# One merged matmul for the up projection's two column blocks, fp32 retention values, a residual transposed on VectorE, and tiles on multiples of 512 bytes

## The chip, the cores and the metric

The kernel runs on one core of a Trainium2 chip. The metric is the device time of one execution in microseconds (us); smaller is better. The program is one launch. All inputs lie in HBM as float32, and the output is float32.

## What is computed

One layer of a decoder over 16 learned meta tokens and 256 real tokens (272 in all), model width 2048:

```python
u = rmsnorm(h, attn_norm)
proj = u @ w_in                      # 2048 x 6144: q, k, v of 8 heads; k, q, v, gate of 4 retention heads
ya = rmsnorm(diff_attention(q, k, v), attn_subln) * 0.8
yr = rmsnorm(retention(rq, rk, rv), ret_norm) * silu(rg)
h = h + concat(ya, yr) @ w_out       # 2048 x 2048
u = rmsnorm(h, ffn_norm)
h = h + (silu(causal_conv3(u @ w_gate)) * (u @ w_up)) @ w_down   # 2048 x 5632 twice, 5632 x 2048
return rmsnorm(h, final_norm)[256 real tokens]
```

The weights are read once, 208 blocks of 1 MB in all.

## The kernel before

**Number format.** Every large product is made in three TensorE matmuls of the type fp32r. An operand x is split into a high part (a cast to fp32r) and a low part (x minus the high part, again fp32r), and the product is high·high + high·low + low·high, all added up in PSUM. `prep` (L99 on ScalarE, L100 on VectorE) splits each half block of weights, 128x1024, into `whi` and `wlo`; there are three buffers of each. `load` (L87, on the SP queue) brings a block of 1 MB into one of three `raw` buffers.

**Projections.** `gemm` (L257) makes one block of 128 output features for all tokens: 16 steps k of 128 input features, and in each step three matmuls, L276 `whi`·`hi`, L277 `whi`·`lo`, L278 `wlo`·`hi`. The weights are the stationary operand (128x128, loaded for each matmul), the activations the moving one. Their width is 272 tokens (keys and values), 258 (queries, gates, the output projection, the FFN gate, which needs two tokens more for the convolution) or 256 (the FFN up projection). The activations lie transposed in SBUF, features on partitions: `xhi`, `xlo` for the input projection, `yhi`, `ylo` for the output projection, `ghi`, `glo` for the FFN. `Halves` is a small class that lets one name stand for two tiles of eight steps each. `big`, `wts`, `y`, `att`, `fw` are pools of SBUF; tiles of one tag share a place.

**Order of the work.** Input projection (48 blocks, with the tasks of attention and retention put between matmuls by `pump`), output projection (16 blocks), then for each f of 44 the gate and the up projection, then the down projection. Each engine takes its instructions in order; the framework settles that order when the program is built, from a simulated timeline.

**Retention** (`ret_tasks`). The scores of a head (`rs`, L420, plain fp32) are multiplied by a decay (L422), then split into `sd` (L423) and `sl` (L424); the values are transposed on TensorE and split into `rvh` (L434) and `rvl` (L435); `av` makes three matmuls for each of three key blocks (L448 to L450), twice for each of four heads.

**Output projection** (L551 and on). After each of 16 blocks j, `hT` is the sum of the projection and the residual (L556); its squares, `ghi` (L563) and `glo` (L564) are made from it. A side task transposes two 128x128 pieces of `hT` on TensorE into `ph` (L570), and ScalarE copies them to `htok` (L571), the residual with tokens on partitions, which the down projection needs.

**FFN** (L587 and on). For each f: `g` = gate·`rstd2` (L590), the convolution (L592, L595), `s` = silu (L598), `u` = up·`rstd2` (L601), `u`·`s` (L602), and the split into `fhi` and `flo` (L603, L604). Behind the loop `fn` (the final norm's weights, in the place of `ghi`'s first half) is loaded on the POOL queue (L611) and scaled on VectorE (L616).

**Down projection** (L621 and on). `fhi` or `flo` is the stationary operand, 512 columns of weights the moving one (L629 to L631, PSUM tile `o`). The last six half blocks of the last 512 columns are held back and used in matmuls of 256 columns (`oe`) for the second token block.

**Places in SBUF.** Added up from the tile sizes in the order of allocation, each 128x128 block of `whi` and `wlo` starts 192 bytes past a multiple of 512 bytes (so 64 past a multiple of 128), and each of `fhi` and `flo` on a multiple of 128. A row of `ghi` or `glo` has 258 x 4 = 1032 bytes, so each step k starts 8 bytes further within a line of 128 bytes; a row of `xhi` has 1088 bytes.

Of the kernel before, what the change touches and what calls it, by code (L numbers as in the profile page):

```python
# [10 lines left out]
F32 = mybir.dt.float32  # L11
F32R = mybir.dt.float32r
# [14 lines left out]
NQ = T - Q0  # L27
QT = NQ // 3
KB = [(0, Q0 + QT), (Q0 + QT, Q0 + 2 * QT), (Q0 + 2 * QT, T)]
AH = 8  # L30
# [13 lines left out]
class Halves:  # L44
    def __init__(self, tiles):
        self.tiles = tiles

    def __getitem__(self, ix):
        p, k = ix[0], ix[1]
        return self.tiles[k // HK][(p, k % HK) + tuple(ix[2:])]  # L50


@with_exitstack
def trunk_kernel(ctx, tc, a, out):
# [5 lines left out]
    wp = ctx.enter_context(tc.tile_pool(name="wts", bufs=1))  # L60
    sp = ctx.enter_context(tc.tile_pool(name="small", bufs=2))

    xhi = Halves([big.tile([P, HK, T], F32R, tag=f"acthi{i}", name=f"xhi{i}")
                  for i in range(2)])
    xlo = big.tile([P, KT, T], F32R, tag="actlo", name="xlo")

# [65 lines left out]
    V.memset(ones, 1.0 / D)  # L132
    one = cp.tile([P, P], F32, name="one")
    V.memset(one, 1.0)
    onesr = cp.tile([P, P], F32R, name="onesr")
    V.tensor_copy(out=onesr, in_=one)
    warm = cp.tile([P, 512], BF16, name="warm")
# [118 lines left out]

    def gemm(idx, hi, lo, t0, n, pumps):  # L257
        if idx < 4:
            return first[idx]
        if idx < 6:  # L260
            ps = misc(f"mm{idx}")
        elif idx == 6:
            ps = psx[:, 1]
        else:
            ps = ps1.tile([P, 512], F32, tag="mm", bufs=3, name=f"mm{idx}")
        for half in range(2):
            hf = 2 * idx + half
            ahead(hf)
            whi, wlo = pairs.pop(hf)
            for kk in range(HK):  # L270
                k = half * HK + kk
                wh = whi[:, kk * P:(kk + 1) * P]
                wl = wlo[:, kk * P:(kk + 1) * P]
                xh = hi[:, k, t0:t0 + n]
                xl = lo[:, k, t0:t0 + n]
                PE.matmul(ps[:, :n], wh, xh, start=(k == 0), stop=False)  # L276
                PE.matmul(ps[:, :n], wh, xl, start=False, stop=False)  # L277
                PE.matmul(ps[:, :n], wl, xh, start=False, stop=(k == KT - 1))  # L278
                if kk == HK // 2 - 1 or kk == HK - 1:
                    pump(pumps)  # L280
        return ps

    with ExitStack() as p1:
        yp = p1.enter_context(tc.tile_pool(name="y", bufs=1))
        ap_ = p1.enter_context(tc.tile_pool(name="att", bufs=2))
        yhi = yp.tile([P, KT, NQ], F32R, name="yhi")
        ylo = yp.tile([P, KT, NQ], F32R, name="ylo")

# [113 lines left out]
        def ret_tasks(r, k, q, vs):  # L402
# [3 lines left out]
            dk = [dt_[:KB[0][1], 0], dt_[:QT, 1, :2 * QT], dt_[:QT, 1, 2 * QT:]]  # L406
            sd = [ap_.tile([P, (3 - j) * QT], F32R, tag=f"at{j}", name=f"sd{r}_{j}")
                  for j in range(3)]
            sl = [ap_.tile([P, (3 - j) * QT], F32R, tag=f"sl{j}", name=f"sl{r}_{j}")
                  for j in range(3)]  # L410
            vh = ap_.tile([P, 3, 2 * P], F32R, tag="q2", name=f"rvh{r}")
            vl = ap_.tile([P, 3, 2 * P], F32R, tag="k2", name=f"rvl{r}")
            st = {}

            def scores(j):
                def f():
# [3 lines left out]
                    PE.matmul(ps[:e - b, :n], k[:, b:e], q[:, j * QT:], start=True, stop=True)  # L420
                    t = ap_.tile([P, NQ], F32, tag="kl", name=f"sdf{r}_{j}")
                    V.tensor_tensor(out=t[:e - b, :n], in0=ps[:e - b, :n], in1=dk[j], op=ALU.mult)  # L422
                    S.copy(out=sd[j][:e - b], in_=t[:e - b, :n])  # L423
                    V.tensor_tensor(out=sl[j][:e - b], in0=t[:e - b, :n],  # L424
                                    in1=sd[j][:e - b].bitcast(F32), op=ALU.subtract)
                return f

            def vtr(j):
                def f():
                    b, e = KB[j]  # L430
                    ps = misc(f"rv{r}_{j}")
                    for c in range(2):
                        PE.transpose(ps[:e - b, c * P:(c + 1) * P], vs[c][:, b:e], idt)
                    S.copy(out=vh[:e - b, j], in_=ps[:e - b, :2 * P])  # L434
                    V.tensor_tensor(out=vl[:e - b, j], in0=ps[:e - b, :2 * P],  # L435
                                    in1=vh[:e - b, j].bitcast(F32), op=ALU.subtract)
                return f

            def av(c):
                def f():  # L440
# [4 lines left out]
                    for j, (b, e) in enumerate(KB):  # L445
                        n = e - b
                        o = y[:, c, j * QT:NQ]
                        PE.matmul(o, vh[:n, j, cs], sd[j][:n], start=(j == 0), stop=False)  # L448
                        PE.matmul(o, vh[:n, j, cs], sl[j][:n], start=False, stop=False)
                        PE.matmul(o, vl[:n, j, cs], sd[j][:n], start=False, stop=(j == 2))  # L450
                    q_ = ap_.tile([P, NQ], F32, tag="A", bufs=3, name=f"rsq{r}_{c}")
# [68 lines left out]
        for kind, r in RSEQ:  # L520
# [16 lines left out]
            for c in range(2):  # L537
# [7 lines left out]

        ghi = Halves([big.tile([P, HK, NQ], F32R, tag=f"acthi{i}", name=f"ghi{i}")
                      for i in range(2)])
        glo = big.tile([P, KT, NQ], F32R, tag="actlo", name="glo")
        htok = big.tile([P, 2, D], F32, tag="htok", name="htok")
        acc2 = yp.tile([P, NQ], F32, name="acc2")  # L550
        for j in range(KT):  # L551
# [14 lines left out]

            def htr(j=j, hT=hT):
                ps = misc(f"ph{j}")
                for m in range(2):
                    PE.transpose(ps[:, m * P:(m + 1) * P], hT[:, 2 + m * P:2 + (m + 1) * P], idt)  # L570
                S.copy(out=htok[:, :, j * P:(j + 1) * P],  # L571
                       in_=ps[:, :2 * P].rearrange("p (m c) -> p m c", m=2))
            side.append(htr)
        pump(len(side))
# [7 lines left out]
    with ExitStack() as p2:  # L582
        fp = p2.enter_context(tc.tile_pool(name="ff", bufs=1))
        fw = p2.enter_context(tc.tile_pool(name="fw", bufs=2))
        fhi = fp.tile([P, NF, SEQ], F32R, name="fhi")
        flo = fp.tile([P, NF, SEQ], F32R, name="flo")
        for f in range(NF):  # L587
            ps = gemm(idx, ghi, glo, 0, NQ, 0)
            g = fw.tile([P, NQ], F32, tag="g", name=f"fg{f}")
# [8 lines left out]
            S.activation(out=s, in_=c, func=AF.Silu)  # L598
            ps = gemm(idx + 1, ghi, glo, 2, SEQ, 0)
            u = fw.tile([P, SEQ], F32, tag="u", name=f"fu{f}")  # L600
            V.tensor_tensor(out=u, in0=ps[:, :SEQ], in1=rstd2[:, 2:], op=ALU.mult)  # L601
            V.tensor_tensor(out=u, in0=u, in1=s, op=ALU.mult)  # L602
# [3 lines left out]
            idx += 2  # L606
        fn = big.tile([P, D], F32, tag="acthi0", name="fn")
        endt = big.tile([P, D], F32R, tag="acthi1", name="endt")
        tailt = big.tile([P, 2 * D], F32R, tag="actlo", name="tailt")
        junk = misc("junk")  # L610
# [185 lines left out]
```

## Time and profile before

| | us |
|---|---|
| runs (3) | 1190.66, 1190.8, 1190.87; median 1190.8 |
| the profiled execution | 1190.21 |
| its span, first to last instruction | 1188.4 |

The profiled execution is the one that every row comes from. Its span is 1.8 us shorter than its time. TensorE's matmuls (PE) and its weight loads (PEld) are shown as two engines; DVE is VectorE, ACT ScalarE, SP the engine whose queue issues most DMAs. Matmuls are pipelined and the ends that the trace gives are modelled, so what a matmul costs in a stream is read from the distance between starts and not from its duration.

### The profile page before, as it was taken

How to read it: one execution, taken by the hardware profiler on the slowest of the kernel's cores; microseconds unless marked ns; L12 is line 12 of the kernel's file. 1: busy time of each engine (PE TensorE's matmuls, PEld its weight loads, DVE VectorE, ACT ScalarE, POOL GpSimd, SP SyncE). 2: the span in 40 equal slices, each digit the busy share in tenths (PEclk: the TensorE clock that was granted, in tenths of full speed). 3: DMA queues.
4: the chain of work that ended last, by engine and by line, in shares of the span. 5: the costliest groups of instructions: out<-in, count | busy, mean ns of one | idle time of the engine just before them, and what ended most of it. 6: DMA issues, size and time to landing. Idle time of an engine off the chain costs nothing.

```text
span 1188.4 us, 21369 instructions
## 1 busy us (share of the span) xinstructions
PE 1176.3 (99%) x8847; PEld 1129.8 (95%) x8847; DVE 788.5 (66%) x1413; ACT 559.4 (47%) x871; POOL 2.0 (0%) x7
## 2 busy tenths in 40 slices
PE   9999999999999999999999999999999999999997
PEld 8999999999999999999999999999999988888886
DVE  7888877677776567666666666666666645454544
ACT  7576665544445544444444444444444434343442
POOL 0000000000000000000000000000000000000000
PEclk9999999999999999999999999999999999999998
DMA  8544444444446555555555555455555654555552
GB/s 300 205 156 144 142 145 168 163 156 151 168 150 213 198 187 180 190 192 185 178 180 184 193 190 178 178 184 191 193 179 177 218 207 177 200 189 186 195 188 105
DMA packets 35970, 215.72 MB, mean 182 GB/s; under 512 B 4322, under 2 KB 8650, under 8 KB 11168
## 3 DMA queue, kind: packets, MB, share of 16 engines
q1 hardware_dynamic: 35584, 213.17, 50.8%
q8 instruction: 69, 1.13, 0.4%
q0 software_dynamic: 144, 1.05, 0.3%
q14 instruction: 29, 0.24, 0.1%
q10 hardware_dynamic: 144, 0.14, 0.0%
HBM read 212.24 MB, written 2.10 MB: 180 GB/s over the span
## 4 chain that ended last, share of the span: by engine, by line
PE 95%; DMA 2%; DVE 2%; issue 0%; ACT 0%; SPq 0%; DVEq 0%; ACTq 0%
PE mm L276 24%; PE mm L278 23%; PE mm L277 23%; PE o L631 7%; PE o L629 7%; PE o L630 7%; DMA raw<-in_w_in_dram 2%; PE po L380 1%; DVE wlo L100 1%; DMA raw<-in_w_first_dram 1%; PE sc L330 0%; PE sc L328 0%; DMA xr<-in_x_dram 0%; PE pa L368 0%; PE rs L420 0%
## 5 line engine op out<-in xcount | busy, mean ns | idle before, releaser
L99 ACT CAST whi<-raw 128x1024 fp32r<-128x1024 f32 x381 | 399.7, 1049 | 545.5 <-PE mm L277 300.0
L100 DVE TENSOR_TENSOR wlo<-raw,whi 128x1024 fp32r<-128x1024 f32 x381 | 466.1, 1224 | 267.8 <-ACT whi L99 264.7
L276 PE MATMUL mm<-ghi,whi 128*128 128x258 f32 (+1 forms) x1408 | 396.9, 282 | 0.0
L278 PE MATMUL mm<-ghi,wlo 128*128 128x258 f32 (+1 forms) x1408 | 396.6, 282 | 0.0
L277 PE MATMUL mm<-glo,whi 128*128 128x258 f32 (+1 forms) x1408 | 396.1, 281 | 0.0
L277 PEld LDWEIGHTS mm<-glo,whi 128*128 128x128 f32 x1408 | 266.4, 189 | 0.0
L276 PEld LDWEIGHTS mm<-ghi,whi 128*128 128x128 f32 x1408 | 266.0, 189 | 0.0
L278 PEld LDWEIGHTS mm<-ghi,wlo 128*128 128x128 f32 x1408 | 265.8, 189 | 0.0
L276 PE MATMUL mm<-xhi,whi 128*128 128x272 f32 (+1 forms) x688 | 200.4, 291 | 0.0
L277 PE MATMUL mm<-xlo,whi 128*128 128x272 f32 (+1 forms) x688 | 198.9, 289 | 0.0
L278 PE MATMUL mm<-xhi,wlo 128*128 128x272 f32 (+1 forms) x688 | 197.9, 288 | 0.5 <-DVE wlo L100 0.5
L631 PE MATMUL o<-whi,flo 128*128 128x512 f32 x334 | 131.2, 393 | 0.0
L630 PE MATMUL o<-wlo,fhi 128*128 128x512 f32 x334 | 130.3, 390 | 0.0
L278 PEld LDWEIGHTS mm<-xhi,wlo 128*128 128x128 f32 x688 | 129.5, 188 | 0.8 <-DVE wlo L100 0.7
L276 PEld LDWEIGHTS mm<-xhi,whi 128*128 128x128 f32 x688 | 129.6, 188 | 0.1
L277 PEld LDWEIGHTS mm<-xlo,whi 128*128 128x128 f32 x688 | 129.6, 188 | 0.1
L629 PE MATMUL o<-whi,fhi 128*128 128x512 f32 x334 | 117.8, 391 | 0.0
L630 PEld LDWEIGHTS o<-wlo,fhi 128*128 128x128 f32 x334 | 62.7, 188 | 14.2
L631 PEld LDWEIGHTS o<-whi,flo 128*128 128x128 f32 x334 | 62.7, 188 | 13.5
L629 PEld LDWEIGHTS o<-whi,fhi 128*128 128x128 f32 x334 | 62.7, 188 | 13.1
L276 PE MATMUL mm<-yhi,whi 128*128 128x258 f32 x256 | 73.2, 288 | 0.4 <-ACT whi L99 0.4
L278 PE MATMUL mm<-yhi,wlo 128*128 128x258 f32 x256 | 72.3, 284 | 0.0
(245 smaller groups left out, 1086.5 us busy)
## 6 DMA issues: line engine op xcount, KB each, us to landing
raw<-in_w_in_dram SPq DMA_DIRECT2D x44, 1024.0 KB, 4.9
raw<-in_w_gate_dram SPq DMA_DIRECT2D x44, 1024.0 KB, 4.8
raw<-in_w_up_dram SPq DMA_DIRECT2D x44, 1024.0 KB, 4.8
raw<-in_w_down_dram SPq DMA_DIRECT2D x44, 1024.0 KB, 4.9
raw<-in_w_out_dram SPq DMA_DIRECT2D x16, 1024.0 KB, 4.9
raw<-in_w_first_dram SPq DMA_DIRECT2D x6, 512.0 KB, 8.2
xres<-in_x_dram SPq DMA_DIRECT2D x16, 129.0 KB, 3.9
xr<-in_x_dram SPq DMA_DIRECT2D x6, 273.0 KB, 7.4
```

What stands on the lines that cost most here:

```text
L99: S.copy(out=hi, in_=src)
L100: V.tensor_tensor(out=lo, in0=src, in1=hi.bitcast(F32), op=ALU.subtract)
L276: PE.matmul(ps[:, :n], wh, xh, start=(k == 0), stop=False)
L277: PE.matmul(ps[:, :n], wh, xl, start=False, stop=False)
L278: PE.matmul(ps[:, :n], wl, xh, start=False, stop=(k == KT - 1))
L380: PE.matmul(ps[:QT, i * P:(i + 1) * P], at[j][:n, i - j], vt[:n, j], start=(j == 0), stop=(j == i))
L629: PE.matmul(o, ah, wh, start=start and kk == 0, stop=False)
L630: PE.matmul(o, ah, wl, start=False, stop=False)
L631: PE.matmul(o, al, wh, start=False, stop=stop and kk == 1)
```

## The change

- **Merged up columns.** `ghi` and `glo` of eight steps now lie in one tile `gs[i]`, `[128, 2, 8, 288]`. In the up projection one matmul of 512 columns streams both (two runs of 256 columns) past one load of `whi` and writes 512 PSUM columns; `wlo`·`hi` is added to the first 256. ScalarE copies the second 256 columns to SBUF (`ul`), VectorE adds the first 256 to them. The factor `rstd2` goes to `s`.
- **Plain fp32 retention values.** `sd` and the values (`vt`) stay fp32 and unsplit; one fp32 matmul stands for three fp32r ones.
- **DVE-transposed residual.** VectorE transposes `hT` in blocks of 32x32 into `hb`; four DMAs write it to a scratch tensor `hd` in HBM in token order (runs of 32 floats), and two DMAs in the FFN loop (before f = 8 and f = 16) load it to `htok`.
- **Places.** Pads (`spad`, `cpad`) and the removal of `one` put the weight tiles on multiples of 512 bytes. Activation rows have 288 columns (1152 bytes), the first token that the up projection reads starts on a multiple of 128 bytes (offsets `XO` and `GO`), so that of the 258-column reads 8 bytes ahead of one. `fn` gets a tile of its own in the place of the closed pool `fw`; `endt` and `tailt` take the places of `gs`.

```diff
+TW = 288
+XO = 32 - META
+GO = 30
...
 class Halves:
-    def __init__(self, tiles):
-        self.tiles = tiles
+    def __init__(self, tiles, off, width, lead=()):
+        self.tiles, self.off, self.width, self.lead = tiles, off, width, lead
+        self.per = KT // len(tiles)
...
-        p, k = ix[0], ix[1]
-        return self.tiles[k // HK][(p, k % HK) + tuple(ix[2:])]
+        k = ix[1]
+        c = ix[2] if len(ix) > 2 else slice(0, self.width)
+        return self.tiles[k // self.per][(ix[0],) + self.lead + (
+            k % self.per, slice(c.start + self.off, c.stop + self.off))]
...
+    spad = sp.tile([P, 16], F32, name="spad", bufs=1)
+    dp = ctx.enter_context(tc.tile_pool(name="dram", bufs=1, space=bass.MemoryType.DRAM))
+    xs = [big.tile([P, 2, HK, TW], F32R, tag=f"act{i}", name=f"x{i}") for i in range(2)]
+    xhi, xlo = Halves(xs, XO, T, (0,)), Halves(xs, XO, T, (1,))
...
-    one = cp.tile([P, P], F32, name="one")
+    cpad = cp.tile([P, 80], F32, name="cpad")
...
-    def gemm(idx, hi, lo, t0, n, pumps):
+    def gemm(idx, hi, lo, t0, n, pumps, both=None):
...
-                PE.matmul(ps[:, :n], wh, xh, start=(k == 0), stop=False)
-                PE.matmul(ps[:, :n], wh, xl, start=False, stop=False)
-                PE.matmul(ps[:, :n], wl, xh, start=False, stop=(k == KT - 1))
+                if both is not None:
+                    xb = both[k // HK][:, :, k % HK, GO + t0:GO + t0 + n]
+                    if k == KT - 1:
+                        PE.matmul(ps[:, :n], wl, xh, start=False, stop=False)
+                    PE.matmul(ps[:, :2 * n], wh, xb, start=(k == 0), stop=(k == KT - 1))
+                    if k < KT - 1:
+                        PE.matmul(ps[:, :n], wl, xh, start=False, stop=False)
+                else:
...
-        yhi = yp.tile([P, KT, NQ], F32R, name="yhi")
+        yhi = Halves([yp.tile([P, KT, TW], F32R, name="yhi")], GO, NQ)
...
-                    t = ap_.tile([P, NQ], F32, tag="kl", name=f"sdf{r}_{j}")
-                    V.tensor_tensor(out=t[:e - b, :n], in0=ps[:e - b, :n], in1=dk[j], op=ALU.mult)
-                    S.copy(out=sd[j][:e - b], in_=t[:e - b, :n])
-                    V.tensor_tensor(out=sl[j][:e - b], in0=t[:e - b, :n],
-                                    in1=sd[j][:e - b].bitcast(F32), op=ALU.subtract)
+                    V.tensor_tensor(out=sd[j][:e - b], in0=ps[:e - b, :n], in1=dk[j],
+                                    op=ALU.mult)
...
-                    S.copy(out=vh[:e - b, j], in_=ps[:e - b, :2 * P])
-                    V.tensor_tensor(out=vl[:e - b, j], in0=ps[:e - b, :2 * P],
-                                    in1=vh[:e - b, j].bitcast(F32), op=ALU.subtract)
+                    S.copy(out=vt[:e - b, j], in_=ps[:e - b, :2 * P])
...
-                        PE.matmul(o, vh[:n, j, cs], sd[j][:n], start=(j == 0), stop=False)
-                        PE.matmul(o, vh[:n, j, cs], sl[j][:n], start=False, stop=False)
-                        PE.matmul(o, vl[:n, j, cs], sd[j][:n], start=False, stop=(j == 2))
+                        PE.matmul(o, vt[:n, j, cs], sd[j][:n], start=(j == 0), stop=(j == 2))
...
+        gs = [big.tile([P, 2, HK, TW], F32R, tag=f"act{i}", name=f"g{i}") for i in range(2)]
+        ghi, glo = Halves(gs, GO, NQ, (0,)), Halves(gs, GO, NQ, (1,))
+        hd = dp.tile([SEQ, D], F32, name="hd")
...
-            def htr(j=j, hT=hT):
-                ps = misc(f"ph{j}")
-                for m in range(2):
-                    PE.transpose(ps[:, m * P:(m + 1) * P], hT[:, 2 + m * P:2 + (m + 1) * P], idt)
-                S.copy(out=htok[:, :, j * P:(j + 1) * P],
-                       in_=ps[:, :2 * P].rearrange("p (m c) -> p m c", m=2))
-            side.append(htr)
+            hb = ap_.tile([P, SEQ], F32, tag="t", name=f"hb{j}")
+            V.transpose(out=hb, in_=hT[:, 2:])
+            for i in range(4):
+                c = j * P + i * 32
+                nc.sync.dma_start(
+                    out=hd[:, c:c + 32].rearrange("(b t) f -> t b f", t=32),
+                    in_=hb[i * 32:(i + 1) * 32].rearrange("t (b f) -> t b f", f=32))
...
         for f in range(NF):
+            if f in (8, 16):
+                m = f // 8 - 1
+                nc.sync.dma_start(out=htok[:, m], in_=hd[m * P:(m + 1) * P])
...
-            ps = gemm(idx + 1, ghi, glo, 2, SEQ, 0)
-            u = fw.tile([P, SEQ], F32, tag="u", name=f"fu{f}")
-            V.tensor_tensor(out=u, in0=ps[:, :SEQ], in1=rstd2[:, 2:], op=ALU.mult)
+            V.tensor_tensor(out=s, in0=s, in1=rstd2[:, 2:], op=ALU.mult)
+            ps = gemm(idx + 1, ghi, glo, 2, SEQ, 0, gs)
+            ul = fw.tile([P, SEQ], F32, tag="ul", name=f"ful{f}")
+            S.copy(out=ul, in_=ps[:, SEQ:])
+            u = ul
+            V.tensor_tensor(out=u, in0=ps[:, :SEQ], in1=ul, op=ALU.add)
             V.tensor_tensor(out=u, in0=u, in1=s, op=ALU.mult)
...
-        fn = big.tile([P, D], F32, tag="acthi0", name="fn")
-        endt = big.tile([P, D], F32R, tag="acthi1", name="endt")
-        tailt = big.tile([P, 2 * D], F32R, tag="actlo", name="tailt")
+        p3.close()
+        fnp = p2.enter_context(tc.tile_pool(name="fnp", bufs=1))
+        fn = fnp.tile([P, D], F32, name="fn")
+        endt = big.tile([P, D], F32R, tag="act0", name="endt")
+        tailt = big.tile([P, 2 * D], F32R, tag="act1", name="tailt")
```

## Rows read from the trace of the kernel before

**Rows 1.** The page, part 1: busy us, share of the span and instructions by engine.
```profile
PE 1176.3 (99%) x8847; PEld 1129.8 (95%) x8847; DVE 788.5 (66%) x1413; ACT 559.4 (47%) x871; POOL 2.0 (0%) x7
```

**Rows 2.** Stretches: length, busy us of PE, PEld, DVE, ACT, POOL, clock, DMA share, GB/s.
```profile
352.00:443.00 91.00, 90.56 (x753) 90.29 (x752) 58.06 (x83) 48.06 (x79) 0.00 (x0) 1.00 0.58 205
443.00:941.00 498.00, 498.00 (x4167) 497.45 (x4167) 336.75 (x489) 214.42 (x262) 0.65 (x1) 1.00 0.53 185
941.00:1180.00 239.00, 238.91 (x1080) 197.31 (x1078) 116.87 (x114) 96.90 (x105) 0.00 (x0) 1.00 0.51 180
```

**Rows 3.** Groups by line and form: operands, shapes, count, busy us, mean ns, idle before.
```profile
L276 PE MATMUL mm<-ghi,whi 128*128 128x258 f32 x704 | 199.3, 283 | 0.0
L276 PE MATMUL mm<-ghi,whi 128*128 128x256 f32 x704 | 197.6, 281 | 0.0
L276 PE MATMUL mm<-xhi,whi 128*128 128x272 f32 x416 | 122.0, 293 | 0.0
L276 PE MATMUL mm<-xhi,whi 128*128 128x258 f32 x272 | 78.4, 288 | 0.0
```

**Rows 4.** PE in time order (start, us): first matmul of a gate, an up, a gate.
```profile
663.28 0.28 PE L276 MATMUL mm<-ghi,whi 128*128 128x258 f32 x1
...
669.03 0.28 PE L276 MATMUL mm<-ghi,whi 128*128 128x256 f32 x1
...
674.73 0.28 PE L276 MATMUL mm<-ghi,whi 128*128 128x258 f32 x1
```

**Rows 5.** PE in time order, down projection: two matmuls twelve apart.
```profile
980.13 0.39 PE L629 MATMUL o<-whi,fhi 128*128 128x512 f32 x1
...
982.88 0.39 PE L629 MATMUL o<-whi,fhi 128*128 128x512 f32 x1
```

**Rows 6.** PE in time order, last matmuls: two eight apart, two 44 apart.
```profile
1168.20 0.28 PE L629 MATMUL oe<-whi,fhi 128*128 128x256 f32 x1
...
1169.14 0.28 PE L629 MATMUL oe<-whi,fhi 128*128 128x256 f32 x1
...
1174.53 0.28 PE L630 MATMUL oe<-wlo,fhi 128*128 128x256 f32 x1
...
1179.52 0.28 PE L630 MATMUL oe<-tailt,fhi 128*128 128x256 f32 x1
```

**Rows 7.** PE in time order, input projection: two 272-column matmuls eleven apart.
```profile
299.75 0.29 PE L276 MATMUL mm<-xhi,whi 128*128 128x272 f32 x1
...
301.15 0.29 PE L278 MATMUL mm<-xhi,wlo 128*128 128x272 f32 x1
```

**Rows 8.** PE in time order, output projection: the transposes and what follows them.
```profile
406.56 0.38 PE L570 MATMUL ph<-c_ident,hT 128*128 128x128 f32 x2
406.69 0.37 PE L276 MATMUL mm<-yhi,whi 128*128 128x258 f32 x1
406.90 0.28 PE L277 MATMUL mm<-ylo,whi 128*128 128x258 f32 x1
```

**Rows 9.** PE in time order: retention scores; one half head, first matmul to the next stream.
```profile
253.61 0.89 PE L420 MATMUL rs<-rq,rk 128*100 128x258 f32 x4
...
269.39 0.28 PE L448 MATMUL ro<-sd,rvh 100*128 100x258 f32 x1
...
270.55 0.29 PE L277 MATMUL mm<-xlo,whi 128*128 128x272 f32 x1
```

**Rows 10.** The SP queue in time order, output projection: loads one block apart.
```profile
409.02 0.33 SPq L87 DMA_DIRECT2D raw<-in_w_out_dram  x1
...
415.03 0.33 SPq L87 DMA_DIRECT2D raw<-in_w_gate_dram  x1
```

**Rows 11.** DVE in time order at the end of the FFN loop; in brackets idle, releaser.
```profile
940.35 0.42 DVE L604 TENSOR_TENSOR flo<-fu,fhi 128x256 fp32r<-128x256 f32 x1
942.75 1.23 DVE L616 TENSOR_SCALAR fn<-fn 128x2048 f32<-128x2048 f32 x1 [1.99 <-DMA fn<-in_final_norm_dram]
```

**Rows 12.** The page, part 6: DMA issues, KB each, median us to landing.
```profile
raw<-in_w_out_dram SPq DMA_DIRECT2D x16, 1024.0 KB, 4.9
```

More of the change, by code (lines that the diff above doesn't have):

```diff
@@ L61, in trunk_kernel @@
     sp = ctx.enter_context(tc.tile_pool(name="small", bufs=2))
-    xhi = Halves([big.tile([P, HK, T], F32R, tag=f"acthi{i}", name=f"xhi{i}")
-                  for i in range(2)])
-    xlo = big.tile([P, KT, T], F32R, tag="actlo", name="xlo")
+    spad = sp.tile([P, 16], F32, name="spad", bufs=1)
+    V.memset(spad, 0.0)
+    dp = ctx.enter_context(tc.tile_pool(name="dram", bufs=1, space=bass.MemoryType.DRAM))
+    xs = [big.tile([P, 2, HK, TW], F32R, tag=f"act{i}", name=f"x{i}") for i in range(2)]
+    xhi, xlo = Halves(xs, XO, T, (0,)), Halves(xs, XO, T, (1,))
     chunks = []
@@ L132, in trunk_kernel @@
     V.memset(ones, 1.0 / D)
-    one = cp.tile([P, P], F32, name="one")
-    V.memset(one, 1.0)
+    cpad = cp.tile([P, 80], F32, name="cpad")
+    V.memset(cpad, 0.0)
     onesr = cp.tile([P, P], F32R, name="onesr")
-    V.tensor_copy(out=onesr, in_=one)
+    V.memset(onesr.bitcast(F32), 1.0)
     warm = cp.tile([P, 512], BF16, name="warm")
@@ L275, in gemm @@
                 xl = lo[:, k, t0:t0 + n]
-                PE.matmul(ps[:, :n], wh, xh, start=(k == 0), stop=False)
-                PE.matmul(ps[:, :n], wh, xl, start=False, stop=False)
-                PE.matmul(ps[:, :n], wl, xh, start=False, stop=(k == KT - 1))
+                if both is not None:
[6 more added lines that the diff above has]
+                else:
+                    PE.matmul(ps[:, :n], wh, xh, start=(k == 0), stop=False)
+                    PE.matmul(ps[:, :n], wh, xl, start=False, stop=False)
+                    PE.matmul(ps[:, :n], wl, xh, start=False, stop=(k == KT - 1))
                 if kk == HK // 2 - 1 or kk == HK - 1:
@@ L285, in trunk_kernel @@
         ap_ = p1.enter_context(tc.tile_pool(name="att", bufs=2))
-        yhi = yp.tile([P, KT, NQ], F32R, name="yhi")
-        ylo = yp.tile([P, KT, NQ], F32R, name="ylo")
+        yhi = Halves([yp.tile([P, KT, TW], F32R, name="yhi")], GO, NQ)
+        ylo = Halves([yp.tile([P, KT, TW], F32R, name="ylo")], GO, NQ)
         def row_rstd(ss, width, name):
@@ L406, in ret_tasks @@
             dk = [dt_[:KB[0][1], 0], dt_[:QT, 1, :2 * QT], dt_[:QT, 1, 2 * QT:]]
-            sd = [ap_.tile([P, (3 - j) * QT], F32R, tag=f"at{j}", name=f"sd{r}_{j}")
+            sd = [ap_.tile([P, (3 - j) * QT], F32, tag=f"at{j}", name=f"sd{r}_{j}")
                   for j in range(3)]
[L409 to L412, printed above, removed]
+            vt = ap_.tile([P, 3, 2 * P], F32, tag="q2", name=f"rvt{r}")
             st = {}
@@ L544, in trunk_kernel @@
         pump(len(side))
[L546 to L549, printed above, removed]
+        gs = [big.tile([P, 2, HK, TW], F32R, tag=f"act{i}", name=f"g{i}") for i in range(2)]
+        ghi, glo = Halves(gs, GO, NQ, (0,)), Halves(gs, GO, NQ, (1,))
+        hd = dp.tile([SEQ, D], F32, name="hd")
         acc2 = yp.tile([P, NQ], F32, name="acc2")
@@ L583, in trunk_kernel @@
         fp = p2.enter_context(tc.tile_pool(name="ff", bufs=1))
-        fw = p2.enter_context(tc.tile_pool(name="fw", bufs=2))
+        htok = big.tile([P, 2, D], F32, tag="htok", name="htok")
         fhi = fp.tile([P, NF, SEQ], F32R, name="fhi")
         flo = fp.tile([P, NF, SEQ], F32R, name="flo")
+        p3 = ExitStack()
+        fw = p3.enter_context(tc.tile_pool(name="fw", bufs=2))
         for f in range(NF):
+            if f in (8, 16):
+                m = f // 8 - 1
+                nc.sync.dma_start(out=htok[:, m], in_=hd[m * P:(m + 1) * P])
             ps = gemm(idx, ghi, glo, 0, NQ, 0)
```

## The prediction

> **What bounds the kernel now.** I read the page first, then the table of stretches, then PE in time order in each stage, and last SP's queue and VectorE around the two places where the change adds a wait.
>
> The page says that PE is busy 99% of the span and its weight loads 95% [rows 1]. Busy is a weak measure for pipelined matmuls, so the reader should look at the stretches [rows 2]. In all three PE has no gap of note and the granted clock is 1.00, which is the upper of the two levels, 2.4 GHz. DVE is busy 58 of 91, 337 of 498 and 117 of 239 us, the DMA engines half of the time. So the sum of the distances between matmul starts sets the end, and nothing else does. The stretches differ in one column: the weight loads are busy 497.45 of 498 us in the FFN, but only 197.31 of 239 us in the down projection. With 258 or 256 streamed columns per load the loader never rests; with 512 it does.
>
> Then the distances. A gate takes 5.75 us from its first matmul to the up's first, an up 5.70 us to the next gate [rows 4]; each has 48 matmuls, so 119.8 ns and 118.8 ns. Twelve matmuls of 512 columns take 2.75 us [rows 5], 229.2 ns each. Eleven steps of 272 columns take 1.40 us [rows 7], 127.3 ns. The last matmuls have 256 columns too, but stationary and moving blocks that all start on the same residues: 44 steps in 4.99 us, 113.4 ns, and eight earlier ones in 0.94 us, 117.5 ns [rows 6]. So the same instruction, at the same clock, costs 113.4, 117.5 or 118.8 ns, and what I can see to differ is where its operands lie, and what came before.
>
> **The change, part by part.** The sum is made against the profiled execution, 1190.2 us (span 1188.4); the median of the runs, 1190.8, is 0.6 above it, and I add that at the end.
>
> *Merged up columns.* There are 704 steps k in the up projections (44 x 16) [rows 3]. Each loses a weight load and a matmul: two of 256 columns, 2 x 118.8 = 237.6 ns, become one of 512, 229.2 ns. That is 8.4 ns a step and 5.9 us. The moving operand is two runs of 256 columns far apart, which no row shows. At best that costs nothing; at worst it eats the 8.4 ns and the gain is 0. I take nothing, the row of 512 columns being the nearest, and keep 0 to 5.9 us. The Trainium skill ("TensorE: Matmul & The Clock Gate", Back-to-back issue gap) gives N/2.4 + 2.5 ns for a warm matmul, so 109.2 ns for 256 columns and 215.8 ns for 512; by it the merge would be worth 2.6 ns a step, an estimate of 1.8 us in place of 5.9. The trace does not agree: both sizes are slower than that here, and the smaller by more.
>
> Behind the merge stand one more ScalarE copy and one more VectorE operation per f, of the kind of the 0.42 us one [rows 11]: 44 x 0.42 = 18.5 us on each engine. DVE has 161 us free in that stretch and ACT 284 [rows 2], and a PSUM tile has three buffers, so this is hidden. Without that cover the chain after each up would be 0.4 us longer, 18 us in all.
>
> *The residual.* The 32 TensorE transposes go. From the first of a pair to the second matmul behind it is 0.34 us where one step would be 0.12 [rows 8], so a pair costs 0.22 us, 16 pairs 3.5 us. In their place are 16 VectorE transposes of 128x256. None is in the trace; bounded by nothing and by the split of 128x1024 values, four times the size, some 1.2 us, I take 0.42 us each, as for an operation of this shape [rows 11], 6.7 us in a stretch where DVE is idle 33 us [rows 2]: hidden. On SP's queue there are 64 new DMA issues, at 0.33 us each [rows 10] 21 us. Per block j that is 1.3 us, behind a wait for the transpose, with the next weight load queued after them. SP issues a load every 6.01 us [rows 10] and is otherwise nearly idle, the load lands in 4.9 us [rows 12], and three blocks of buffer stand between load and use, so even a load 2 us late comes in time. The engines of DMA are 58% busy in this stretch [rows 2]; 2 MB more in 91 us add about a ninth to 205 GB/s. The pieces are 128 bytes, and the Trainium skill ("DMA: Bandwidth & Descriptors", Specifications) says that below 512 bytes a write is read, changed and written back; no row here shows what such a piece costs. If these writes took all of the idle 42%, weight loads would start to come late; I count nothing.
>
> *Retention.* Nine matmuls of a half head take, from the first to the second step behind them, 1.16 us [rows 9], less one 272-column step 1.03 us. In fp32 each matmul is issued as two. Four of these, of 258 and 172 columns, show 0.89 us [rows 9], the drain of the last included; with two more of 86 columns, at most 0.22 us by two weight loads' distance of some 0.11, the new half head is 0.8 to 1.1 us. Eight of them: between 2 us won and 1 us lost. I take 0. The ACT and DVE work that goes is hidden now.
>
> *Places.* This is the large unknown. After the change every step k starts on the same residue and the weights on multiples of 512 bytes. The stationary blocks now lie 64 bytes past a multiple of 128 where the distance is 118.8, 119.8 and 127.3 ns, and on a multiple of 128 where it is 113.4 and 117.5. I take the middle of those two, 115.5 ns, for 256 and 258 columns, because that is the nearest row in form; the bounds are 113.4 ns, and no change. Gate: 2112 matmuls x 4.3 = 9.1 us. The up's third matmul: 704 x 3.3 = 2.3 us. Output projection: 6.01 us less 0.22 over 48 [rows 8, 10] is 120.6 ns, 768 x 5.1 = 3.9 us. Input projection, 258 columns: 3 x 272 [rows 3] = 816 at the gate's 119.8, 816 x 4.3 = 3.5 us. With 272 columns, 3 x 416 = 1248 matmuls, there is no aligned row; scaled by columns from 113.4 ns the floor is 120.5, so 0 to 6.8 ns each. I take 4 ns, 5.0 us. The down projection had its stationary side on 128 already: 0. Sum 23.8 us, between 0 and 36.5 (gate 13.5, third matmul 3.8, output 5.5, input 5.2 and 8.5).
>
> *The rest.* `fn` can now be loaded only after the last operation of the FFN loop, at 940.8 us, where the old load was already on its way: DVE waited 1.99 us for it [rows 11]. A VectorE wait that is some 5 us longer would hold the next split of weights, if the order of instructions stays. The framework settles that order anew; I count 0 and keep 4 us once.
>
> Sum: 5.9 + 3.5 + 0 + 23.8 = 33.2; 1190.2 - 33.2 + 0.6 = 1157.6, say 1158 us.
>
> **Rivals.**
>
> *Places do nothing.* The distance is set by something that alignment does not touch. For it: the 272-column rows already start on multiples of 64 bytes and are not better for it (127.3 ns against a scaled 126.3 from 118.8). The 117.5 ns steps [rows 6] lie on the good residues and are still slow. Against it: 44 steps in a row at 113.4. Then only 5.9 + 3.5 is left: 1181 us, and 1187 if the two-run operand eats the merge.
>
> *Slower: all steps fall on the slow residue.* Today the distance is a mean over changing residues. With all rows on one residue every matmul of a kind takes the same distance, and nothing says that it is the short one; eight steps in a row at 117.5 show that a slow pattern can hold itself. If it lay as far above 118.8 as 113.4 lies below, 5.4 ns on 5648 matmuls (2112 + 704 + 768 + 816 + 1248) cost 30.5 us: 1190.8 + 30.5 - 9.4 = 1212. It decides as soon as the mean rises by 9.4 us / 5648 = 1.7 ns.
>
> *A transfer in the way.* The residual's small writes delay weight loads in the output projection, or the late `fn` holds VectorE. In the worst case each of 16 blocks waits the 1.3 us that its four DMAs are issued in, 21 us; with `fn` 4 us. On top of places that work that is about 1183. Against it: the buffers above.
>
> **How the numbers follow.** Places work: 0.55, 1158 us, of its own from 1145 (all at the floor, 36.5 in place of 23.8 us) to 1171 (all at 117.5 and no gain at 272 columns: 2112 x 2.3 + 704 x 1.3 + 768 x 3.1 + 816 x 2.3 = 10.0 us). Places do nothing: 0.25, 1181 (to 1187). Slow residue: 0.11, 1212. A transfer: 0.09, 1183, some of it above today's time. The range is 1147 to 1187: it leaves out the slow residue, and about 0.06 from the edges of the others, the lowest 2 us of the likeliest case among them. A difference of 0.2% (2.4 us) is about what a measurement of this kernel can tell from none. Faster by more: 0.55 + 0.24 + 0.07 = 0.86; within it 0.03; slower 0.11.
>
> **What would show it.** Merge: the 512-column matmuls of the up stand 229 ns from the next start, and an up takes some 16 x (229 + 115.5) = 5.51 us in place of 5.70. With the old distance for the third matmul it is 5.57. Places: a gate takes 48 x 115.5 = 5.54 us in place of 5.75, and the distances are equal from step to step. Residual: no `ph`, the output projection's period goes from 6.01 to 5.54 us, and SP's loads keep that pace. `fn`: DVE's wait before its scaling and any PE gap near 945 us. The prediction is wrong if a gate still takes 5.75 us or more (places), if a 512-column step with two runs takes 237 ns or more (merge), or if PE shows gaps behind weight splits in the output projection.

## The result, and the profile after

The changed kernel takes 1181.7 us (median of 4 runs, 1180.9 to 1182.3) against 1190.7 us (1190.4 to 1190.9) beside it: a ratio of 0.9925, 95% interval 0.9912 to 0.9937, 9.1 us. The direction and the range of the prediction held, its size did not: 33 us were forecast. The time is that of the rival "places do nothing" (1181), but the experiments show that this rival's sentence is not true either.

The page of the changed kernel, part 1, then its table of stretches (columns as in [rows 2]; output projection, FFN, down projection):

```profile
PE 1168.3 (99%) x8087; PEld 1093.1 (93%) x8087; DVE 804.0 (68%) x1450; ACT 564.0 (48%) x887; POOL 2.0 (0%) x7
```

```profile
351.00:438.00 87.00, 86.09 (x704) 85.37 (x704) 62.88 (x96) 43.72 (x64) 0.00 (x0) 1.00 0.76 228
438.00:932.00 494.00, 494.00 (x3472) 464.19 (x3471) 351.41 (x534) 225.66 (x304) 0.00 (x0) 1.00 0.54 190
932.00:1172.00 240.00, 240.00 (x1094) 200.12 (x1093) 119.46 (x118) 98.83 (x108) 0.65 (x1) 1.00 0.52 184
```

760 matmuls and as many weight loads are gone. The clock is still 1.00, and in these stretches PE idles 0.9 us in the output projection (0.4 in [rows 2]) and nowhere else, so the distances between starts still set the end, and the time has to be looked for in them. One f of the FFN, PE in time order (start, us): a gate's last matmul, the first two steps of an up, the first matmul of the next gate, the first of the next up:

```profile
664.96 0.28 PE L294 MATMUL mm<-g,wlo 128*128 128x258 f32 x1
665.09 0.40 PE L288 MATMUL mm<-g,whi 128*128 128x512 f32 x1
665.44 0.40 PE L288 MATMUL mm<-g,whi 128*128 128x512 f32 x1
...
670.66 0.28 PE L292 MATMUL mm<-g,whi 128*128 128x258 f32 x1
...
676.47 0.39 PE L288 MATMUL mm<-g,whi 128*128 128x512 f32 x1
```

The up takes 5.57 us (5.70 in [rows 4]), the gate 5.81, and 5.80 in the mean over all f, where [rows 4] had 5.75. The forecast was 5.54 for the gate. The last matmuls, two of them 44 apart as in [rows 6]:

```profile
1166.56 0.28 PE L645 MATMUL oe<-wlo,fhi 128*128 128x256 f32 x1
...
1171.83 0.28 PE L645 MATMUL oe<-tailt,fhi 128*128 128x256 f32 x1
```

That is 5.27 us or 119.8 ns each, in place of 113.4. The fastest steps of the old kernel, on which the prediction built its term, have become slow ones.

From the first matmul of each stage to that of the next, before and after: input projection 331.8 and 331.7 us, output projection 96.7 and 94.7, FFN 504.3 and 500.7, down projection (to the start of the last matmul) 241.6 and 239.8.

The side paths are hidden but for some 0.5 us, the added idle time of PE, which waits for weight splits at the start of the output projection. SP's queue in the output projection, one block apart (5.82 us; [rows 10] had 6.01), and the transposes and writes of the residual by tile, then the page's DMA issues:

```profile
401.95 0.35 SPq L95 DMA_DIRECT2D raw<-in_w_out_dram  x1
403.05 0.35 SPq L558 DMA_DIRECT2D xres<-in_x_dram  x1
403.53 1.84 SPq L576 DMA_DIRECT2D hd<-hb  x4
407.77 0.35 SPq L95 DMA_DIRECT2D raw<-in_w_out_dram  x1
```

```profile
L573 DVE STREAM_TRANSPOSE hb<-hT x16: 404/446/448, 351.4 to 432.1; 128x256 f32<-128x256 f32 x16
```

```profile
raw<-in_w_out_dram SPq DMA_DIRECT2D x16, 1024.0 KB, 5.0
hd<-hb SPq DMA_DIRECT2D x64, 32.0 KB, 3.7
```

A weight load lands in 5.0 us (4.9 in [rows 12]), a VectorE transpose takes 0.45 us, and a block takes 48 x 121.0 ns = 5.81 us: nothing else is in it. The wait for `fn` on VectorE is 0.88 us, where [rows 11] had 1.99:

```profile
941.06 1.23 DVE L631 TENSOR_SCALAR fn<-fn 128x2048 f32<-128x2048 f32 x1 [0.88 <-DMA fn<-in_final_norm_dram]
```

### The profile page after: what moved, and what is told of

Its sections match the earlier page's. It is cut to its first block, busy times and chain, and to the rows that moved or that the text cites. A ratio compares the mean times of both kernels' runs of the same rounds, so it can differ in the third digit from the quotient of the medians.

```text
span 1180.1 us, 19961 instructions
## 1 busy us (share of the span) xinstructions
PE 1168.3 (99%) x8087; PEld 1093.1 (93%) x8087; DVE 804.0 (68%) x1450; ACT 564.0 (48%) x887; POOL 2.0 (0%) x7
## 4 chain that ended last, share of the span: by engine, by line
PE 97%; DMA 1%; DVE 1%; ACT 0%; issue 0%; SPq 0%; DVEq 0%; ACTq 0%
PE mm L292 17%; PE mm L293 17%; PE mm L294 17%; PE mm L288 14%; PE mm L290 7%; PE o L645 7%; PE o L646 7%; PE o L644 7%; PE po L396 1%; PE ro L456 1%; DMA raw<-in_w_first_dram 1%; PE mm L213 1%; PE mm L211 1%; PE mm L212 1%; PE mm L287 0%; PE sc L346 0%
## 5 line engine op out<-in xcount | busy, mean ns | idle before, releaser
L288 PE MATMUL mm<-g,whi 128*128 128x512 f32 x704 | 249.1, 392 | 0.0
L292 PE MATMUL mm<-x,whi 128*128 128x272 f32 (+1 forms) x688 | 200.2, 291 | 0.0
L293 PE MATMUL mm<-g,whi 128*128 128x258 f32 x704 | 199.8, 284 | 0.0
L292 PE MATMUL mm<-g,whi 128*128 128x258 f32 x704 | 199.4, 283 | 0.0
L293 PE MATMUL mm<-x,whi 128*128 128x272 f32 (+1 forms) x688 | 199.2, 290 | 0.0
L294 PE MATMUL mm<-g,wlo 128*128 128x258 f32 x704 | 198.8, 282 | 0.0
L294 PE MATMUL mm<-x,wlo 128*128 128x272 f32 (+1 forms) x688 | 197.4, 287 | 0.8 <-DVE wlo L108 0.8
L290 PE MATMUL mm<-g,wlo 128*128 128x256 f32 x660 | 185.2, 281 | 0.0
L288 PEld LDWEIGHTS mm<-g,whi 128*128 128x128 f32 x704 | 132.1, 188 | 26.1
L293 PEld LDWEIGHTS mm<-g,whi 128*128 128x128 f32 x704 | 132.4, 188 | 1.9
L294 PEld LDWEIGHTS mm<-g,wlo 128*128 128x128 f32 x704 | 132.9, 189 | 0.0
L292 PEld LDWEIGHTS mm<-g,whi 128*128 128x128 f32 x704 | 132.4, 188 | 0.0
L294 PEld LDWEIGHTS mm<-x,wlo 128*128 128x128 f32 x688 | 129.6, 188 | 1.0 <-DVE wlo L108 1.0
L293 PEld LDWEIGHTS mm<-x,whi 128*128 128x128 f32 x688 | 129.7, 189 | 0.1
L292 PEld LDWEIGHTS mm<-x,whi 128*128 128x128 f32 x688 | 129.7, 188 | 0.1
L290 PEld LDWEIGHTS mm<-g,wlo 128*128 128x128 f32 x660 | 124.3, 188 | 0.0
```

The source lines that it names most:

```text
L288: PE.matmul(ps[:, :2 * n], wh, xb, start=(k == 0), stop=(k == KT - 1))
L290: PE.matmul(ps[:, :n], wl, xh, start=False, stop=False)
```

## The experiments

The question was whether the places do nothing, or do things that cancel. Below, a pair (m, s) is the byte address modulo 128 at which the moving and the stationary operand begin, and the pitch is the distance between the rows of consecutive steps k. In the changed kernel the gate, q and the output projection are at (120, 0), the up at (0, 0), the 272 columns at (64, 0), all at a pitch of 1152 bytes. A distance is the mean from start to start within one kind and stage, gaps behind other work left out; in a map each pair has a stretch of 16 steps of its own, and its distance is the mean behind the stretch's first matmuls, good to some 0.2 ns. Edits are shown shortened.

**A map of the pairs.** TensorE's stream by itself, other engines idle.

```
X = cp.tile([P, 2, 16, 320], F32R)        # pitch 1280
for n, m, w in CONFIGS:
    for k in range(16):                   # three matmuls a step, as in gemm
        PE.matmul(ps[:, :n], W[:, 0, w + k * P:w + (k + 1) * P],
                  X[:, 0, k, m:m + n], ...)
```

> A kernel of TensorE streams alone, which computes nothing of the reference: 128 stretches of 48 matmuls in the pattern of a projection (high weights with high and low activations, low weights with high activations), each stretch with another byte residue, modulo 128, of the moving and of the stationary operand; 256, 258, 272 and 512 columns. Theory 1, the places of the two operands set the distance: it depends on the residues, with stretches of 256 columns at 113 ns and others at 118 to 125 ns, and the pair of the changed kernel (moving 0, stationary 0) is among the slow ones, 120 ns. Theory 2, places do nothing and the distance comes from what the other engines and the DMAs do at the time: with all of them idle every stretch of one width shows one distance, some 113 ns at 256 columns.

256 columns, PE in time order, two matmuls 24 apart at (64, 0) and then at (64, 64):

```profile
67.67 0.28 PE L124 MATMUL ps<-X,W 128*128 128x256 f32 x1
...
70.39 0.28 PE L124 MATMUL ps<-X,W 128*128 128x256 f32 x1
...
158.94 0.28 PE L124 MATMUL ps<-X,W 128*128 128x256 f32 x1
...
161.82 0.28 PE L124 MATMUL ps<-X,W 128*128 128x256 f32 x1
```

2.72 / 24 = 113.3 ns and 2.88 / 24 = 120.0 ns for the same instruction at the same clock. (0, 64) and (112, 0) take 113.3 too, (0, 0) 120.0, the rest 116.7 to 121.5. These are paces that a stretch settles into: (112, 0) first has twelve matmuls of 114 to 130 ns. What counts is how the two operands lie to each other, not that either is aligned, and their difference isn't all of it: (32, 96) takes 117.7. With 512 moving columns, in the pattern of the down projection, equal places take 226.7, (64, 0) 229.1, most others 233.4. 258 columns never come below 116.6, and the merged step takes 346.6 to 353.4.

**The change without its places.** Rows at their own length, no offsets, the old pads; merge, residual and retention stay.

```
-TW = 288
-XO = 32 - META
-GO = 30
+TWX, TWG, XO, GO = T, NQ, 0, 0
-    cpad = cp.tile([P, 80], F32, name="cpad")
```

> The changed kernel with its places undone: rows of 272 and 258 columns, no offsets, the old pads; merge, fp32 values and the residual's path stay. Theory 1 (the places made the gate's step 1.1 ns dearer and the down projection's 2.1 ns cheaper, and the two cancel): a gate takes 5.745 us again, a down step 228.9 ns, and the time is 1181 to 1183 us. Theory 2 (places do nothing at all): 1181 to 1182 us with gates as in the changed kernel, 5.80 us. Rival: the places won some 10 us or more and another part of the change lost them: 1190 us or above.

1182.5 us (1182.2 to 1184.3), ratio 0.9932 [0.9919, 0.9944]. PE in time order, gate, up, gate:

```profile
658.73 0.28 PE L291 MATMUL mm<-g,whi 128*128 128x258 f32 x1
...
664.46 0.39 PE L287 MATMUL mm<-g,whi 128*128 128x512 f32 x1
...
670.08 0.28 PE L291 MATMUL mm<-g,whi 128*128 128x258 f32 x1
```

Gate 5.73 and up 5.62, means 5.737 and 5.617. So the places by themselves give 1182.5 - 1181.7 = 0.8 us (0.7 if each is taken against the old kernel that ran beside it), within what can be told from nothing, and by kind of matmul they are six terms of both signs: gate 44 x +59 ns = +2.6 us, up 44 x -43 ns = -1.9, down -1.8, 272 columns 1248 x -0.7 ns = -0.9, q 816 x +1.0 ns = +0.8, output projection 768 x +0.8 ns = +0.6.

**The merge alone**, in the kernel before. It needs the halves in one tile, so the low half of `g` lies 8256 bytes behind the high one, 64 past a multiple of 128; the places are the old ones but for that, as in the run above.

```
+PE.matmul(ps[:, :2 * n], wh, xb, start=(k == 0), stop=(k == KT - 1))
-PE.matmul(ps[:, :n], wh, xh, start=(k == 0), stop=False)
-PE.matmul(ps[:, :n], wh, xl, start=False, stop=False)
```

> The kernel before with the merged up columns alone. By the term of the sum 704 steps at 8.4 ns, 5.9 us: 1184.9 us. If the two runs of the moving operand eat the gain: 1190.8 us. An up takes 5.57 us.

1187.0 us (1186.2 to 1188.2) against 1190.9 beside it, ratio 0.9969 [0.9957, 0.9980]: 3.9 us. The up goes from 5.701 to 5.617 us, 44 x 84 ns = 3.7. Two runs of 256 columns take 232.4 ns there, and not the 229.2 of one run of 512.

**The residual alone**, in the kernel before.

```
-PE.transpose(ps[:, m * P:(m + 1) * P], hT[:, 2 + m * P:2 + (m + 1) * P], idt)
+V.transpose(out=hb, in_=hT[:, 2:])
+nc.sync.dma_start(out=hd[:, c:c + 32]..., in_=hb[i * 32:(i + 1) * 32]...)   # 4 a block
```

> The kernel before with the residual's new path alone (VectorE transposes, writes of 128-byte runs, two loads). By the term of the sum 16 pairs of transposes at 0.22 us, 3.5 us: 1187.3 us. If the small writes or the wait on the queue cost part of it, some 2 us are left: 1188.8 us, with PE gaps in the first blocks of the output projection.

1187.3 us (1186.4 to 1187.9) against 1190.9, ratio 0.9968 [0.9956, 0.9981]: 3.6 us. In the trace the output projection goes from 96.7 to 94.0 us, and PE idles the same 0.9 us at its start as in the changed kernel.

**Two more maps, at the kernel's pitch of 1152 bytes.** The row length 288 in place of 320, the halves laid out as in the kernel; the first with 258 columns over both places, the second with 272, 256 and merged columns.

> TensorE streams alone again (nothing of the reference is computed), now with the rows of the changed kernel (1152 bytes, low block 9216 bytes behind the high one): 128 stretches of 48 matmuls of 258 columns, moving residue in steps of 8 bytes, stationary residue in steps of 16. Theory 1 (the pair of residues sets the distance): the pair of the changed kernel's gate, moving 120 and stationary 0, shows the gate's 120.7 ns with all other engines idle; other pairs lie between 116 and 124 ns. Theory 2 (another engine or the DMAs set the gate's distance): that pair shows 117.7 ns, as in the first map, whose rows were 1280 bytes apart.

> The same for 272 columns (moving residues 0 to 48), 256 columns and the merged pair of 512 and 256 columns, at rows of 1152 bytes. Theory 1: 256 columns at moving 64, stationary 0 stay at 113.3 ns and at 0, 0 at 120 ns; the merged step at 0, 0 shows the changed kernel's 348.3 ns, and no merged step falls below three unmerged ones at 113.3 ns, 340 ns. Theory 2: the merged step is nowhere above 343 ns, so that 512 columns are what counts, not the residue.

The stream alone takes 121.1 ns at the gate's pair (the kernel 120.7), 348.0 for the merged step at (0, 0) (the kernel 348.3), 118.9 with 258 columns at (56, 0). So these paces of the kernel are the stream's own; no other engine and no transfer is needed for them. But 256 columns at (64, 0), two matmuls of the second map 24 apart:

```profile
214.66 0.28 PE L118 MATMUL ps<-X,W 128*128 128x256 f32 x1
...
217.49 0.28 PE L118 MATMUL ps<-X,W 128*128 128x256 f32 x1
```

2.83 / 24 = 117.9 ns where the pitch of 1280 gave 113.3. The expectation that 113.3 stays was wrong: the pitch counts as well.

What ran just before counts too. Four pairs stand twice in the second map, behind different pairs, and two of them differ. (64, 64), two matmuls 48 apart, behind (112, 48) and then behind (56, 64):

```profile
259.44 0.28 PE L117 MATMUL ps<-X,W 128*128 128x256 f32 x1
...
265.09 0.28 PE L117 MATMUL ps<-X,W 128*128 128x256 f32 x1
...
442.15 0.28 PE L117 MATMUL ps<-X,W 128*128 128x256 f32 x1
...
447.86 0.28 PE L117 MATMUL ps<-X,W 128*128 128x256 f32 x1
```

5.65 / 48 = 117.7 ns and 5.71 / 48 = 119.0, and in the second half of each stretch still 117.8 and 118.9; (112, 0) has 119.0 and 117.8. So a price in these maps can be off by some 1.2 ns through what came before, which is far less than the 6.7 ns between (64, 0) and (0, 0) in the first.

**The up at (64, 0), not merged**, in the changed kernel.

```
-GO = 30
+GO = 14
-ps = gemm(idx + 1, ghi, glo, 2, SEQ, 0, gs)
+ps = gemm(idx + 1, ghi, glo, 2, SEQ, 0)
```

> The changed kernel without the merge (the up projection in three matmuls of 256 columns, as before) and with the activations of the FFN and the output projection moved 64 bytes, so that the up reads on moving residue 64 against stationary 0. Theory 1: an up takes 48 x 113.3 = 5.44 us in place of 5.57, a gate (moving 56) 5.70 to 5.80; 1176 us, between 1172 and 1181: the merge is worth less than the residue. Theory 2 (the merge is what won, and places do nothing): an up takes 5.70 us again, and the time is 1187 us.

1183.4 us (1183.2 to 1183.7), ratio 0.9939 [0.9926, 0.9953]. The up takes 5.649 us, 117.7 ns a matmul: the map's price at this pitch, and the forecast of this run fell with the one above.

**Even rows first.** With 1152 bytes the place moves by 128 modulo 256 from step to step, with 1280 it does not. Taking the even rows of a half first and then the odd ones makes it constant within each group of four steps: a map, the changed kernel, and the kernel of the last run.

```
+ORD = (0, 2, 4, 6, 1, 3, 5, 7)
-            for kk in range(HK):
+            for i, kk in enumerate(ORD):
```

> TensorE's stream alone again, other engines idle, nothing of the reference computed: rows 1152 bytes apart as in the changed kernel, but in each half of a group the even rows first and then the odd ones, so that from one step to the next the operand moves by 2304 bytes, a multiple of 256. Theory 1 (the rate needs an unchanged place modulo 256 from step to step): the distances of the first map return: 256 columns at residues (64,0) 113.3 to 113.9 ns in place of 117.8, 258 columns at (120,0) 117.7 in place of 121.1 and at (16,0) 116.6, 272 columns at (0,0) 125, the merged step at (0,0) 347.6. Rival (the odd rows, which lie 128 bytes off, have a price of their own that the first map did not sample): the mean stays at the 117.8 and 121.1 of the second and third maps, with the first four steps of a half differing from the last four.

> The changed kernel with the eight steps of a half taken in the order 0 2 4 6 1 3 5 7; nothing else. Theory 1: gate 117.7 to 118 ns a matmul in place of 120.7 (5.65 us for 5.796), up 347.6 a step, output projection 117.7 to 118 in place of 121.0, the 258 columns of the input projection likewise, the 272 columns 126.7 in place of 125.3: 1181.7 - 6.0 - 2.4 - 2.2 + 1.7, about 1173 us. Rival: 1181 to 1182 us with the stages unchanged.

> The same order of steps in the kernel with the up matmuls apart again and gate and up at residues 56 and 64. Theory 1: up 48 x 113.3 to 114 = 5.44 to 5.49 us in place of 5.649, gate 119.3 to 119.6 in place of 120.5, output projection 119.3, input 258 columns 117.7: about 1183.4 - 8.5 - 2.0 - 0.7, 1171 to 1173 us, some 10 us under the changed kernel. Rival: 1183 us with the stages unchanged.

1178.5 us (1177.9 to 1179.3), ratio 0.9900 [0.9885, 0.9914], and 1177.5 us (1177.2 to 1177.9), ratio 0.9890 [0.9873, 0.9906]: 3.2 and 5.9 us better than their own bases, and neither theory's number. The kernel follows the map for the gate (119.3 in both) and the merged step (351.6, map 350 to 351). In the map 256 columns at (64, 0) stay at 117.7, and 258 at (120, 0) take 119.3. Only at (0, 64) does the map look as theory 1 has it, and there just for the even rows: 113.8 in the four even steps of the second half, 117.8 in its four odd ones. The last kernel's up, at (64, 0), does not follow the map. It takes 115.9 ns in place of 117.7; first matmuls of its four groups of four steps, and of the next gate (1.41, 1.37, 1.41 and 1.37 us):

```profile
662.01 0.28 PE L293 MATMUL mm<-g,whi 128*128 128x256 f32 x1
...
663.42 0.28 PE L293 MATMUL mm<-g,whi 128*128 128x256 f32 x1
...
664.79 0.28 PE L293 MATMUL mm<-g,whi 128*128 128x256 f32 x1
...
666.20 0.28 PE L293 MATMUL mm<-g,whi 128*128 128x256 f32 x1
...
667.57 0.28 PE L293 MATMUL mm<-g,whi 128*128 128x258 f32 x1
```

Over all f the groups of even rows take 117.8 ns a matmul, those of odd rows 114.0: theory 1's pace, in half of the steps. So rows 128 bytes off have a price of their own, and a constant place modulo 256 is not by itself the rule.

**The pitch of 1280 in the kernel.** The last two runs take the first map's pitch (the output projection keeps 1152), with the up not merged and some tiles moved to make room. They differ from each other only in the places.

```
-TW = 288
+TW = 320
-XO = 32 - META        # 272 columns at (64, 0)
+XO = 28               # (112, 0); in the other run as it was
-GO = 30               # gate (120, 0), up (0, 0)
+GO = 14               # (56, 0), (64, 0); in the other run as it was
```

> The whole kernel with the row pitch of the first map: token columns of the input projection and of gate and up 1280 bytes apart, weights as in the changed kernel, up matmuls apart, residual path and retention as changed; gate at residue 56, up at 64, the 272 columns at 112 and q's 258 at 40; the output projection stays at a pitch of 1152, residue 56. Room for it: the FFN's scratch tiles single instead of double, the final norm's row, the bias and the last weights in tiles freed earlier. Theory 1 (pitch and residue of the pair set the rate, whatever the other engines do): the first map's prices: up 48 x 113.3 = 5.44 us, gate 48 x 119.3 = 5.73, 272 columns 123.3, q 120.0, output projection 119.1: against the changed kernel -5.9 -3.1 -2.5 -0.5 -1.5, 1168 us. Rival (the prices of a lone stream don't hold in the kernel, because transposes, attention matmuls or the other engines' accesses disturb the settled pattern): up stays near 117.7 ns, 1179 us or more.

> The same kernel with only the residues changed: gate at 120, up at 0, the 272 columns at 64, q's 258 at 120, so the places of the changed kernel on the pitch of 1280; output projection as in the run beside it. Theory 1: gate 48 x 117.7 = 5.65 us, up 48 x 120.0 = 5.76, 272 columns 126.7, q 117.7: 1168 + 10.8 = about 1179 to 1182 us, and up slower here than there by 6.7 ns a matmul while gate is faster by 1.6. Rival: no difference between the two runs beyond 2 us.

1171.5 us (1171.2 to 1172.0), ratio 0.9838 [0.9824, 0.9851], and 1184.4 us (1183.6 to 1187.1), ratio 0.9947 [0.9935, 0.9960]. PE in time order, up, gate, up of the first:

```profile
658.22 0.28 PE L293 MATMUL mm<-g,whi 128*128 128x256 f32 x1
...
663.66 0.28 PE L293 MATMUL mm<-g,whi 128*128 128x258 f32 x1
...
669.42 0.28 PE L293 MATMUL mm<-g,whi 128*128 128x256 f32 x1
```

and gate, up, gate of the second:

```profile
659.58 0.28 PE L294 MATMUL mm<-g,whi 128*128 128x258 f32 x1
...
665.35 0.28 PE L294 MATMUL mm<-g,whi 128*128 128x256 f32 x1
...
671.03 0.29 PE L294 MATMUL mm<-g,whi 128*128 128x258 f32 x1
```

The up takes 5.44 us in one and 5.68 in the other, 113.3 and 118.3 to 118.5 ns; the gate 5.76 and 5.77. Between two kernels that differ in offsets alone lie 12.9 us, where 10.8 were expected. The up's price held in the first; the gate's, 119.3 and 117.7 alone, is 120.0 and 120.1 in the kernels, so that part of theory 1 fell. The first is the fastest version here: 10 us below the changed kernel and 19 below the one before, and it has no merge.

Distances in ns, stream alone and in a kernel:

| columns, pair, pitch | alone | kernel |
|---|---|---|
| 256, (64, 0), 1280 | 113.3 | 113.3 |
| 256, (64, 0), 1152 | 117.8 | 117.7 |
| 256, (0, 0), 1280 | 120.0 | 118.5 |
| merged step, (0, 0), 1152 | 348.0 | 348.3 |
| 258, (120, 0), 1152 | 121.1 | 120.7 (gate) |
| 258, (56, 0), 1152 | 118.9 | 119.1 (output projection), 120.6 (gate) |
| 258, (56, 0), 1280 | 119.3 | 120.0 |
| 258, (120, 0), 1280 | 117.7 | 120.1 |
| 272, (112, 0), 1280 | 123.3 | 124.5 |
| 272, (64, 0), 1280 | 126.7 | 126.5 |
| 512, (0, 0); stationary rows at 1280, in the kernel 1024 | 226.7 | 226.7 |
| 512, (64, 0); the same | 229.1 | 228.9 |

Seven of the twelve rows agree within 0.5 ns, and one more in one of its two stages; the largest miss is 2.4 ns.

## Why the prediction was wrong

*What bounds the kernel.* Right. Every gain and loss found is a distance between matmul starts at a clock of 1.00.

*Places, 23.8 us: the step that failed.* The prediction compared the matmuls at 113.4 ns in [rows 6] with the slower ones and took as the difference that their stationary blocks begin on a multiple of 128. It did not look at the moving side. In the kernel before, the moving weights of those steps begin 64 bytes past such a multiple, while the activations, which are stationary there, begin on one: the pair (64, 0), with a difference of 64. The change puts both on 0, a pair that the first map, at its pitch, prices at 120.0, and exactly these 44 matmuls went from 113.4 to 119.8. (These places are added up from the tile sizes; no trace shows an address.) The eight at 117.5 in the same rows stand among 512-column matmuls; what sets them was not tried. The same edit made the 512-column matmuls of the down projection, which were costed at nothing, 2.2 ns faster: -1.8 us. The gate, forecast at 115.5 ns, stands at 120.7; 2112 x 5.2 = 11 us of the 23 are missing there alone, and the prediction's own sign of being wrong, a gate of 5.75 us or more, came true. The 272 columns, for which 4 ns were taken, gained 0.7. Measured by itself the term is 0.8 us.

*The rivals.* "Places do nothing" gave the right total for a wrong reason: places move a matmul of 256 columns by 6 ns, and by 12.9 us in all between the last two runs. Its 127.3 ns for 272 columns was one row (the stage's mean is 126.1), and the scaled value beside it is 126.2, not 126.3. "All steps on the slow residue" named what happened to the gate (+1.2 ns), but with a mean of about nothing over the stages it did not decide.

*Merge, 5.9 us.* The mechanism was right, the size was not: 3.7 us at the old places, because the matmul of two runs takes 232.4 ns and not 229.2. Whether the two runs or their places make these 3.2 ns was not separated. At the new places a step takes 348.3 and the up gains 44 x 127 ns = 5.6 us; 1.9 of them are the up's term among the places above. By the second map three separate matmuls take 353.4 at that pair, so the merge by itself is again worth about 5 ns a step. The formula of the Trainium skill ("TensorE: Matmul & The Clock Gate", Back-to-back issue gap), which that section gives for an isolated matmul, would have the merge worth 1.8 us by the prediction's estimate; that is too little in both. No run comes down to its 109.2 ns for 256 columns; the least is 113.3.

*Residual, 3.5 us.* Right: 3.6 by the medians, 2.7 in its own stage of the trace. Its small writes are hidden, though not free. In the output projection the DMA engines are busy 0.76 of the time in place of 0.58 [rows 2], for 228 GB/s in place of 205. Share and bytes do not rise together, which agrees with the Trainium skill ("DMA: Bandwidth & Descriptors", Specifications) on writes below 512 bytes. That such a write is read back first is not shown: the bytes read, on the pages before and after, rise by just the 2.1 MB of the two loads.

```profile
HBM read 212.24 MB, written 2.10 MB: 180 GB/s over the span
```

```profile
HBM read 214.34 MB, written 4.19 MB: 185 GB/s over the span
```

*Retention, 0, and the rest.* Merge and residual alone sum to 7.5 us, with retention and without places 8.4 are saved; the difference of 0.9 is less than can be told from nothing. Retention was not run by itself, but the changed kernel's trace has its half heads:

```profile
270.69 1.08 PE L456 MATMUL ro<-sd,rvt 100*128 100x258 f32 x6
271.56 0.37 PE L292 MATMUL mm<-x,whi 128*128 128x272 f32 x1
271.77 0.28 PE L293 MATMUL mm<-x,whi 128*128 128x272 f32 x1
```

That is 1.08 us to the second matmul behind it, where [rows 9] had 1.16: eight times 0.08 are 0.6 us won, inside the forecast of 2 won to 1 lost. `fn` did not delay anything.

*What stays open.* Why a given pair, pitch and order take what they take. It is not the alignment of either operand, not their difference modulo 128 alone, and not by itself a constant place modulo 256. Many prices of the lone stream carry into a kernel (113.3, 117.7, 348, 226.7), others are off by up to 2.4 ns; what came just before moves a price by 1.2 ns in one map, so it may be part of that, but no run set it up to find out. Nor were places modulo 256 and beyond, or the PSUM tiles, held alike in maps and kernels.

## What to carry to other kernels

When PE has no gaps and the clock is full, the distance between starts is a quantity to tune, and it belongs to the pair of operands and the pitch from step to step: measure it on the stream by itself, for the layout that the kernel will have, and then in the kernel, before rounding anything to a "nice" multiple. A row of a profile that looks like the aligned case is evidence only if both operands lie as they will lie after the change. And a sum near zero over several stages should be taken apart by stage before it is read as "no effect".

## What was not expected of the hardware

One matmul of 256 fp32r columns at the full clock takes from 113.3 to 121.5 ns at one pitch with nothing but the two start addresses changed, and 258 columns from 116.6 to 123.3, never the 113.3 of 256. With 1152 in place of 1280 bytes between the rows of consecutive steps the pair (64, 0) loses 4.5 ns, 4%, and the range is 116.6 to 125.5. Beginning both operands on a multiple of 128 bytes is one of the slow choices for 256 columns (120.0 at the pitch of 1280) and the fast one for 512 (226.7).
